# A hybrid decoder block on one core: weights ahead of x at the start, five low-part subtractions moved from GpSimd to VectorE, one weight split read from SBUF

## The chip, the cores and the metric

One core of a Trainium2 chip. The time is the device time of one execution in microseconds (us); less is better. Engines: PE (TensorE, matmuls; PEld are its weight loads), ACT (ScalarE), DVE (VectorE), POOL (GpSimd), SP (SyncE, which issues most transfers). SBUF is the on-chip memory, PSUM the matmuls' accumulators (8 banks).

## The reference, cut to what matters

```python
h = rms_norm(x, norm1_g)                 # x: 512 tokens x 2048
proj = h @ w_in                          # 2048 x 3840, split into head groups
out_a = dilated_mixture(aq, ak, av)      # A: 8 heads x 64
out_b = conformer_conv(bu, bg, ...)      # B: 512 channels
out_c = band_attention(cq, ck, cv, 127, sinks)  # C: 16 query heads, 2 kv heads
x = x + concat([out_a, out_b, out_c]) @ w_out   # 2048 x 2048
h2 = rms_norm(x, norm2_g)
x = x + (silu(h2 @ w_gate) * (h2 @ w_up)) @ w_down   # hidden width 5632
```

All in float32.

## The kernel before, in words

Everything is transposed: channels on the 128 partitions, 512 tokens in the free dimension. A float32 product is made of three matmuls in a reduced format (`mm3`): each operand is written as a rounded high part (a cast on ACT) and the low part that is left (a subtraction on DVE or POOL); high by high, and the two mixed products, are added up in PSUM.

The order of the work is the order in which the program is written; each engine takes its own instructions in that order. `Ticks` is a clock of the program's text: steps are put down for a later tick and written out between the matmuls.

Weights come in *units* of 128 x 1024 (the first two of 128 x 512). `pump` issues their transfers on SP's queue, `split_up_to(u)` writes the cast and the subtraction of all units up to u, and `next_unit` hands out the next one and splits two ahead (`SPLIT_AHEAD`). From the gate projection on the matrices are multiplied by a Strassen-like scheme of seven products, whose weight units are blocks and sums of blocks (`11`, `12`, `21`, `22`, `s`; the sums are made on POOL, L200). A unit there is cast twice on ACT: into PSUM (`wn`, L293), which the subtraction reads, and into SBUF (`wh`, L294), which PE reads. The first four units of that part are still split in the plain way (L289, L290), with one cast into SBUF.

The change touches four places:

- The start. `load_first(k)` loads 128 rows of x, `scaled` multiplies them by the norm's gain on ACT and makes the low part on DVE (L419, L420). The loop over `k` multiplies 16 such blocks into four PSUM banks `g4`, one for each 128 tokens, twelve matmuls a block; the square of x is summed on POOL.
- `split_mix`, which splits the attention's output rows (`mix_c0` and so on, 16 rows in the order of `ROWS`) into `mh_` and `ml_`. For the c rows the subtraction is on POOL (L865).
- `split_rows(k)`, which is called ahead of row k of the output projection and splits the rows k to k+2 that are there by then. `first_two` multiplies the first eight rows, all c rows, for two output tiles at once.
- The limit in `split_up_to` (L287) up to which units are split in the plain way: 93 units of the projections (`units`) and four more.

Around the second and third place ACT, DVE and POOL also do the attention of the A heads: exponentials (`e`), their sums on DVE (L775) and scaling on POOL (L779), transposes on PE (`a1t`), and the preparation of the last key and query tiles (`ak3`, `aq3`).

Of the kernel before, what the change touches and what calls it, by code (L numbers as in the profile page):

```python
# [9 lines left out]
F32 = mybir.dt.float32  # L10
F32R = mybir.dt.float32r
I32 = mybir.dt.int32
AF = mybir.ActivationFunctionType
ALU = mybir.AluOpType

P = 128
T = 512
NT = T // P
D = 2048
KT = D // P  # L20
# [28 lines left out]
ROWS = "c0 c1 c2 c4 c5 c3 c7 c6 a0 a1 b2 b1 b0 b3 a2 a3".split()  # L49
# [73 lines left out]
def kernel(ctx: ExitStack, tc: tile.TileContext, xT, wi, wo, wgu, wd, cst_in, outT):  # L123
    nc = tc.nc
# [20 lines left out]
    def slot(name, dt=F32, cols=T):  # L145
        return sp.tile([P, cols], dt, name=name, tag="s")

    def wide(i, name, dt=F32):
        return xp.tile([P, 2 * T], dt, name=name, tag=f"x{i}")
# [8 lines left out]
    units = [wi[0][:, :T], wi[0][:, T:]] + [wi[u] for u in range(1, 2 * N_IN)]  # L158
# [9 lines left out]
    def take(buf, key, n=1024):  # L168
        assert buf not in held
        held[buf] = key  # L170
        if buf[0] == "x":
            raws[key] = (wide(int(buf[1]), f"w{key}"), n)
        else:
            raws[key] = (wp.tile([P, 1024], F32, name=f"w{key}", tag=f"raw{buf}", bufs=1), n)
        return raws[key][0]

    def drop(key):
        for buf in [b for b, k in held.items() if k == key]:
            held.pop(buf)
        return raws.pop(key)  # L180
# [90 lines left out]
    def pump(limit):  # L271
        while at["entry"] < len(entries) and len(raws) < limit and entries[at["entry"]][0] not in held:
            buf, key, parts = entries[at["entry"]]
            (part,) = parts
            n = part.shape[-1] * (part.shape[1] if len(part.shape) == 3 else 1)
            t = take(buf, key, n)[:, :n]
            nc.sync.dma_start(t if len(part.shape) == 2 else t.rearrange("p (n c) -> p n c", n=part.shape[1]), part)
            at["entry"] += 1

    def split_up_to(i):  # L280
        while at["split"] <= min(i, len(works) - 1):
            key, last, eng = works[at["split"]]
            t, n = drop(key) if last else raws[key]
            u = at["split"]
            hi = wp.tile([P, 1024], F32R, name=f"wh{u}", tag="hi", bufs=SPLIT_BUFS)
            lo = wp.tile([P, 1024], F32R, name=f"wl{u}", tag="lo", bufs=SPLIT_BUFS)
            if eng or u < len(units) + 4:  # L287
                eng = eng or nc.vector
                nc.scalar.copy(hi[:, :n], t[:, :n])  # L289
                eng.tensor_sub(lo[:, :n], t[:, :n], hi[:, :n].bitcast(F32))  # L290
            else:
                near = psum["high"].tile([P, 1024], F32R, name=f"wn{u}", tag="h")
                nc.scalar.copy(near[:, :n], t[:, :n])  # L293
                nc.scalar.copy(hi[:, :n], t[:, :n])  # L294
                nc.vector.tensor_sub(lo[:, :n], t[:, :n], near[:, :n].bitcast(F32))  # L295
            splits[u] = (hi, lo)
            at["split"] += 1
# [5 lines left out]
    def next_unit(ahead=SPLIT_AHEAD):  # L303
        sums_now()
        u = at["use"]
        at["use"] += 1
        split_up_to(u + ahead)
        pump(RAW_EARLY if u < 20 else RAW_BUFS + N_WIDE)
        return splits.pop(u)

    def mm3(out, wh, wl, xh, xl, start, stop):
        nc.tensor.matmul(out, wh, xh, start=start, stop=False)  # L312
        nc.tensor.matmul(out, wh, xl, start=False, stop=False)  # L313
        nc.tensor.matmul(out, wl, xh, start=False, stop=stop)  # L314
# [6 lines left out]
    def load_first(k):  # L321
        x = slot(f"x{k}")
        nc.sync.dma_start(x, xT[k])
        xs.append(x)

    for k in range(X_AHEAD):
        load_first(k)
        u = k if k < 2 else k // 2 + 1
        if u < RAW_EARLY and (k < 2 or k % 2 == 0):
            pump(u + 1)  # L330
# [16 lines left out]
    def col(i):  # L347
        return cst[:, i:i + 1]
# [64 lines left out]
    def scaled(x, g, tag, k):  # L413
        if k < N_WIDE:
            both = wide(k, f"{tag}{k}", F32R)
            hi, lo = both[:, :T], both[:, T:]
        else:
            hi, lo = slot(f"{tag}h{k}", F32R), slot(f"{tag}l{k}", F32R)
        nc.scalar.activation(hi, x, AF.Copy, scale=g)  # L419
        nc.vector.scalar_tensor_tensor(lo, x, g, hi.bitcast(F32), op0=ALU.mult, op1=ALU.subtract)  # L420
        return hi, lo

    def add_square(acc, x, k, tag, eng=nc.gpsimd):
        if k == 0:
            nc.scalar.activation(acc, x, AF.Square)
        else:
            sq = slot(f"{tag}{k}")
            nc.scalar.activation(sq, x, AF.Square)  # L428
            eng.tensor_add(acc, acc, sq)  # L429
# [12 lines left out]
    g4 = [(column if j < COLUMN_BANKS - 1 else bank)(f"in{j}") for j in range(HEAD4)]  # L442
    h_hl = {}
    for k in range(2):
        h_hl[k] = scaled(xs[k], col(C_G1 + k), "h", k)
        split_up_to(k)
    pump(RAW_EARLY)
    add_square(ssum, xs[0], 0, "sq")
    for k in range(KT):
        if k + 2 < KT:  # L450
            h_hl[k + 2] = scaled(xs[k + 2], col(C_G1 + k + 2), "h", k + 2)
        if k < 2 or k % 2 == 0:
            wh, wl = next_unit()
            o = 0
        if k + X_AHEAD < KT:
            load_first(k + X_AHEAD)
        if k == 4:
            nc.sync.dma_start(cst[:, C_G2:], cst_in[:, C_G2:])
        if k + 1 < KT:
            add_square(ssum, xs[k + 1], k + 1, "sq")  # L460
        hi, lo = h_hl.pop(k)
        h_hi.append(hi)
        h_lo.append(lo)
        for i in range(NT):
            s = slice(i * P, (i + 1) * P)
            mm3(g4[i], hi[:, s], lo[:, s], wh[:, o:o + T], wl[:, o:o + T], k == 0, k == KT - 1)
        o += T
    xs = None
    c64 = cp.tile([P, NT], F32, name="c64")
# [79 lines left out]
    def ln_out(mix):  # L549
        b = spread(ln["r"], "lrs")  # L550
        for j in range(NB):
            nc.vector.tensor_mul(yconv[j], yconv[j], b)
        for j in range(NB):
            nc.scalar.activation(yconv[j], yconv[j], AF.Silu, bias=col(C_LB + j), scale=col(C_LG + j))
            mix[f"b{j}"] = yconv[j]
        for n, name in enumerate(r for r in ROWS if r[0] == "b"):
            ticks.after(1 + n, split_mix, name)
# [157 lines left out]
    def attention(kind, box, mix, mi, heads):  # L715
# [7 lines left out]
        def head(h):  # L723
# [107 lines left out]
            def out_rows(b):  # L831
                m = st["mix"]
                nc.vector.tensor_add(m[HALF[h]], m[HALF[h]], b[HALF[h]])
                if h == 1:
                    mix[mi] = m
                    if late:
                        ticks.after(1, split_mix, mi)
# [22 lines left out]
    def split_mix(name):  # L860
        if name not in m_hi:
            m = mix.pop(name)
            hi, lo = slot(f"mh_{name}", F32R), slot(f"ml_{name}", F32R)
            nc.scalar.copy(hi, m)
            (nc.gpsimd if name[0] == "c" else nc.vector).tensor_sub(lo, m, hi.bitcast(F32))  # L865
            m_hi[name], m_lo[name] = hi, lo

    vd = tc.dram_tile([NT, P, T], F32, name="vd")
# [9 lines left out]
    g4 = b = None  # L878
# [126 lines left out]
            operand(q, j, src)  # L1005

    def split_rows(k):
        for name in ROWS[k:k + 3]:
            if name in mix:
                split_mix(name)  # L1010

    def first_two(*ns):
        two = [((bank if i else column)(f"o0_{n}"), *next_unit(SPLIT_AHEAD - i)) for i, n in enumerate(ns)]
        for k in range(8):
            row = ROWS[k]
            while row not in m_hi and row not in mix:
                ticks.tick()
            split_rows(k)
            s = slice(k * P, (k + 1) * P)
            for b, wh, wl in two:  # L1020
                mm3(b, wh[:, s], wl[:, s], m_hi[row], m_lo[row], k == 0, k == 7)
            ticks.tick()
        for i, n in enumerate(ns):
            residual(n, two[i][0], 0)
            load_x(i + 2)
# [4 lines left out]
    for half in range(2):  # L1030
        for i, n in enumerate(OUT_ORDER[half]):
# [9 lines left out]
            wh, wl = next_unit()  # L1041
            if half == 1 and i == KT - 1:
                drop(first_sum[0][1])
            for kk in range(8):
                if half == 1 and i == KT - 2 and kk == 4:
                    first_sum[0][0]()
                k = 8 * half + kk
# [4 lines left out]
                s = slice(kk * P, (kk + 1) * P)  # L1052
# [345 lines left out]
    for g in range(2 * NP + N_DOWN):  # L1398
        t = g - 2 * NP
        turned = 0 <= t < N_TURNED  # L1400
        if t < 0:
            p, m = GU_ORDER[g // 2], g % 2
# [4 lines left out]
        for i, q in enumerate(ORDER):  # L1407
            sums_now()
            run(evacs)
            for sub in range(BY // 2 if turned else 1):  # L1410
                w = next_unit(SPLIT_AHEAD - (g == 0 and i == 2))
# [124 lines left out]
```

## Time and profile before

| | |
|---|---|
| three runs | 1879.63 us median, 1879.41 to 1881.6 |
| profiled execution | 1879.36 us, span 1877.5 us |
| PE busy | 1871.7 us, 9848 matmuls |
| DVE, ACT, POOL busy | 1454.1, 1343.7, 1217.0 us |
| chain that ended last | PE 96% of the span |
| granted TensorE clock | 1.0 |

A row of the timeline gives start and duration in us, the engine, the line of the kernel, the operation, what it writes and reads, and in brackets the idle time of the engine before it with what ended it. PE's records overlap by some tenths of a microsecond, since matmuls are pipelined.

### The profile page before, as it was taken

What the parts mean: (1) busy time and instruction counts of PE and PEld (TensorE: products, weight loads), DVE (VectorE), ACT (ScalarE), POOL (GpSimd) and SP (SyncE); (2) the same over time, 40 slices, a digit from 0 to 9 for tenths busy, and PEclk for the clock granted to TensorE, in tenths of its full rate; (3) what the DMA queues carried; (4) which work ended last, traced back from release to release, by engine and by line L of the source; (5) the groups of instructions that cost most, each with busy time, mean ns of one, the idle gap of its engine ahead of it and who ended that gap; (6) DMA issues with size and microseconds to landing.
All of it is one profiled execution on the core that took longest, in us unless ns stands there. A gap on an engine that the chain in (4) does not pass through costs nothing.

```text
span 1877.5 us, 28557 instructions
## 1 busy us (share of the span) xinstructions
PE 1871.7 (100%) x9848; PEld 1609.1 (86%) x9848; DVE 1454.1 (77%) x2376; ACT 1343.7 (72%) x1883; POOL 1217.0 (65%) x812
## 2 busy tenths in 40 slices
PE   9999999999999999999999999999999999999999
PEld 7888888888888888888888888888888888888888
DVE  7578999897679777777777777777777677778887
ACT  6246655553466887888878888888888887777675
POOL 5023444362155887778878877888787767766786
PEclk9999999999999999999999999999999999999999
DMA  7333233333342354443544445344455475578984
GB/s 271 122 109 102 81 105 102 121 107 138 113 146 89 114 178 142 163 163 132 184 134 164 162 137 181 132 166 160 145 175 196 151 237 185 196 253 283 311 241 124
DMA packets 157986, 301.09 MB, mean 160 GB/s; under 512 B 29968, under 2 KB 69008, under 8 KB 157840
## 3 DMA queue, kind: packets, MB, share of 16 engines
q1 hardware_dynamic: 157696, 299.25, 48.8%
q8 instruction: 78, 1.28, 0.3%
q14 instruction: 68, 0.56, 0.1%
q10 hardware_dynamic: 144, 0.01, 0.0%
HBM read 241.27 MB, written 50.33 MB: 155 GB/s over the span
## 4 chain that ended last, share of the span: by engine, by line
PE 96%; DVE 1%; issue 1%; ACT 1%; POOL 1%; DMA 0%; SPq 0%; DVEq 0%; POOLq 0%; ACTq 0%
PE out L1125 51%; PE out L1267 16%; PE o L313 3%; PE o L314 3%; PE o L312 3%; PE cq L312 1%; PE cq L313 1%; PE cq L314 1%; PE in L313 1%; PE ak L312 1%; PE bg L312 1%; PE ak L314 1%; PE ak L313 1%; PE bu L312 1%; PE bu L314 1%; PE bg L313 1%
## 5 line engine op out<-in xcount | busy, mean ns | idle before, releaser
L1125 PE MATMUL out<-h,wh 128*128 128x512 f32 x2464 | 588.4, 391 | 0.0
L1125 PEld LDWEIGHTS out<-h,wh 128*128 128x128 f32 x2464 | 452.7, 188 | 87.5
L1125 PEld LDWEIGHTS out<-h,wl 128*128 128x128 f32 x2464 | 316.2, 191 | 12.4 <-DVE wl L295 0.4
L1125 PE MATMUL out<-h,wl 128*128 128x256 f32 x2464 | 320.3, 283 | 0.2 <-DVE wl L295 0.2
L1267 PE MATMUL out<-wh,a 128*128 128x512 f32 x896 | 221.3, 389 | 0.0
L1267 PEld LDWEIGHTS out<-wh,a 128*128 128x128 f32 x896 | 168.2, 188 | 34.9
L289 ACT CAST wh<-w 128x1024 fp32r<-128x1024 f32 (+1 forms) x93 | 96.7, 1042 | 125.0 <-PE o L313 43.3
L290 DVE TENSOR_TENSOR wl<-w,wh 128x1024 fp32r<-128x1024 f32 (+1 forms) x93 | 117.2, 1262 | 46.7 <-ACT wh L289 45.7
L1267 PE MATMUL out<-wl,a 128*128 128x512 f32 x448 | 119.7, 389 | 0.0
L1267 PEld LDWEIGHTS out<-wl,a 128*128 128x128 f32 x448 | 84.1, 188 | 17.4
L513 DVE SCALAR_TENSOR_TENSOR y<-bu,cst,y 128x511 f32<-128x511 f32 (+14 forms) x120 | 90.3, 753 | 0.7
L1125 PE MATMUL out<-a,wh 128*128 128x512 f32 x330 | 80.1, 391 | 0.0
L1125 PEld LDWEIGHTS out<-a,wh 128*128 128x128 f32 x330 | 60.2, 188 | 11.4
L312 PE MATMUL o<-mh_c,wh 128*128 128x512 f32 x128 | 51.2, 400 | 0.0
L313 PE MATMUL o<-ml_c,wh 128*128 128x512 f32 x128 | 50.1, 392 | 0.4 <-POOL ml_c L865 0.3
L314 PE MATMUL o<-mh_c,wl 128*128 128x512 f32 x128 | 50.1, 391 | 0.0
L1312 DVE TENSOR_TENSOR Y<-Y,out 128x512 f32<-128x512 f32 x48 | 30.8, 683 | 19.0 <-PE out L1267 18.9
L1125 PEld LDWEIGHTS out<-a,wl 128*128 128x128 f32 x330 | 43.3, 191 | 2.2
L1125 PE MATMUL out<-a,wl 128*128 128x256 f32 x330 | 44.0, 283 | 0.0
L429 POOL TENSOR_TENSOR ssum<-ssum,sq 128x512 f32<-128x512 f32 x15 | 26.6, 1770 | 19.3 <-ACT sq L428 18.8
L312 PE MATMUL cq<-hh,wh 128*128 128x512 f32 x96 | 38.6, 402 | 0.0
L314 PE MATMUL cq<-hh,wl 128*128 128x512 f32 x96 | 37.5, 391 | 0.0
(3111 smaller groups left out, 5197.0 us busy)
## 6 DMA issues: line engine op xcount, KB each, us to landing
od<-a SPq DMA_DIRECT2D x140, 256.0 KB, 4.7
a<-od SPq DMA_DIRECT2D x140, 256.0 KB, 6.2
w<-in_wi SPq DMA_DIRECT2D x59, 512.0 KB, 3.6
w<-in_wo SPq DMA_DIRECT2D x32, 512.0 KB, 3.6
x<-in_xT SPq DMA_DIRECT2D x16, 256.0 KB, 6.7
xr<-in_xT SPq DMA_DIRECT2D x16, 256.0 KB, 3.8
x2d<-xr SPq DMA_DIRECT2D x16, 256.0 KB, 2.0
yd<-z SPq DMA_DIRECT2D x16, 256.0 KB, 5.5
```

The lines of the kernel that those rows point to most:

```text
L289: nc.scalar.copy(hi[:, :n], t[:, :n])
L290: eng.tensor_sub(lo[:, :n], t[:, :n], hi[:, :n].bitcast(F32))
L312: nc.tensor.matmul(out, wh, xh, start=start, stop=False)
L313: nc.tensor.matmul(out, wh, xl, start=False, stop=False)
L314: nc.tensor.matmul(out, wl, xh, start=False, stop=stop)
L429: eng.tensor_add(acc, acc, sq)
L513: nc.vector.scalar_tensor_tensor(yconv[j][:, i:], hconv[j][:, :T - i], c, yconv[j][:, i:], op0=ALU.mult, op1=ALU.add)
L1125: nc.tensor.matmul(out, lhs[:, s], rhs, start=begin, stop=last and low == flip[0] and x is xs[-1], skip_group_check=True)
L1267: nc.tensor.matmul(to[h], x[:, h * P:(h + 1) * P], v[:, j], start=sub == 0 and h not in started, stop=sub == 1 and n in (len(todo) - 1, le ...
L1312: nc.vector.tensor_add(t, t, b)
```

## The change

```diff
@@ split_up_to
-            if eng or u < len(units) + 4:
+            if eng or u < len(units) + 5:
@@ ahead of the loads of x
+    pump(1)
     for k in range(X_AHEAD):
         load_first(k)
@@ scaled
-        nc.scalar.activation(hi, x, AF.Copy, scale=g)
+        for s in (slice(0, P), slice(P, T)) if k == 0 else (slice(0, T),):
+            nc.scalar.activation(hi[:, s], x[:, s], AF.Copy, scale=g)
@@ the first two blocks
     for k in range(2):
+        split_up_to(k)
         h_hl[k] = scaled(xs[k], col(C_G1 + k), "h", k)
-        split_up_to(k)
@@ the loop over k
+        if k == 0:
+            for x, w in ((hi, wh), (hi, wl), (lo, wh)):
+                for i in range(NT):
+                    nc.tensor.matmul(g4[i], x[:, i * P:(i + 1) * P], w[:, :T], start=x is hi and w is wh, stop=False)
+            continue
         for i in range(NT):
             s = slice(i * P, (i + 1) * P)
-            mm3(g4[i], hi[:, s], lo[:, s], wh[:, o:o + T], wl[:, o:o + T], k == 0, k == KT - 1)
+            mm3(g4[i], hi[:, s], lo[:, s], wh[:, o:o + T], wl[:, o:o + T], False, k == KT - 1)
@@ split_mix
-            (nc.gpsimd if name[0] == "c" else nc.vector).tensor_sub(lo, m, hi.bitcast(F32))
+            (nc.gpsimd if name in ROWS[3:6] else nc.vector).tensor_sub(lo, m, hi.bitcast(F32))
@@ split_rows
-        for name in ROWS[k:k + 3]:
+        for name in ROWS[k:k + 4]:
```

`ROWS[3:6]` are c4, c5 and c3. The unit that the new limit takes in is block `12` of the first gate group (unit 97).

At the start the transfer of the first weights is issued ahead of x, and on ACT the casts of the first two units go ahead of the scaling of the first two blocks, the first of which is done in two pieces. ACT's instructions at the start of the program, before:

```order
L419 ACTIVATE h0_143<-x0_77,cst_75 128x512
L289 CAST wh0_146<-w0_79 128x512
L419 ACTIVATE h1_150<-x1_81,cst_75 128x512
L289 CAST wh1_153<-w1_83 128x512
L425 ACTIVATE ssum_138<-x0_77 128x512
L419 ACTIVATE h2_162<-x2_85,cst_75 128x512
L289 CAST wh2_165<-w2_87 128x1024
```

And of the change:

```order
L289 CAST wh0_143<-w0_77 128x512
L421 ACTIVATE h0_147<-x0_79,cst_75 128x128
L421 ACTIVATE h0_147<-x0_79,cst_75 128x384
L289 CAST wh1_151<-w1_83 128x512
L421 ACTIVATE h1_155<-x1_81,cst_75 128x512
L427 ACTIVATE ssum_138<-x0_79 128x512
L421 ACTIVATE h2_163<-x2_85,cst_75 128x512
L289 CAST wh2_166<-w2_87 128x1024
```

Each scaling of the first two blocks now stands behind a cast of weights. The matmuls of block 0 go through the four token groups once for each of the three products, and no longer through the three products for each group.

On DVE, ahead of the output projection, before (`wl63` is a weight unit's low part, `a1e` and `a2e` exponentials, `a2s` scores, `ak3` the last key tile):

```order
L290 TENSOR_TENSOR wl63_4120<-w63_3545,wh63_4119 128x1024
L750 ISA a2s01_4084,a2d0_3780<-a2s01_4084,bias_a_122 128x384
L750 ISA a2d0_3780 128x1
L753 SCALAR_TENSOR_TENSOR a2d0_3780<-a2d0_3780,aq2r_3921 128x1
L775 SCALAR_TENSOR_TENSOR a2e00_4159,a2d0_3780<-a2e00_4159,mult_a_121 128x128
```

And of the change:

```order
L290 TENSOR_TENSOR wl63_4121<-w63_3546,wh63_4120 128x1024
L872 TENSOR_TENSOR ml_c2_4128<-mix_c2_2447,mh_c2_4127 128x512
L757 ISA a2s01_4085,a2d0_3781<-a2s01_4085,bias_a_122 128x384
L757 ISA a2d0_3781 128x1
L760 SCALAR_TENSOR_TENSOR a2d0_3781<-a2d0_3781,aq2r_3922 128x1
L782 SCALAR_TENSOR_TENSOR a2e00_4164,a2d0_3781<-a2e00_4164,mult_a_121 128x128
```

The subtraction of c2 came in; those of c0 and c1 stand some twenty rows further up, those of c7 and c6 behind the two rows of `ak3` that follow (L635, now L642). POOL keeps c4, c5 and c3, which follow one another directly.

On DVE at the gate projection's first units, before (`out` are PSUM banks, `g1r` and `g1u` results of the first group):

```order
L1138 TENSOR_TENSOR g1r_6081<-g1r_6081,out0_5953 128x256
L1139 TENSOR_TENSOR g1r_6081<-g1r_6081,out0_5953 128x256
L295 TENSOR_TENSOR wl97_6086<-w('12', 'g1')_5686,wn97_6087 128x1024
L295 TENSOR_TENSOR wl98_6092<-w('22', 'g1')_5538,wn98_6093 128x1024
L1138 TENSOR_TENSOR g1u_6050<-g1u_6050,out3_5956 128x256
```

And of the change:

```order
L1145 TENSOR_TENSOR g1r_6082<-g1r_6082,out0_5954 128x256
L1146 TENSOR_TENSOR g1r_6082<-g1r_6082,out0_5954 128x256
L290 TENSOR_TENSOR wl97_6087<-w('12', 'g1')_5687,wh97_6086 128x1024
L295 TENSOR_TENSOR wl98_6091<-w('22', 'g1')_5539,wn98_6092 128x1024
L1145 TENSOR_TENSOR g1u_6051<-g1u_6051,out3_5957 128x256
```

Its place is the same; its second input is now `wh97` in SBUF, where it was `wn97` in PSUM, and ACT's cast of `wn97` is gone.

## The prediction

> **What bounds the kernel now.** I read the page first, then the timeline of the three places that the change touches: the first 13 us, the stretch from 390 to 414 us where the output projection begins, and the one from 577 to 609 us where the gate projection begins. Two lines of the page give the frame.
>
> ```profile
> span 1877.5 us, 28557 instructions
> PE 1871.7 (100%) x9848; PEld 1609.1 (86%) x9848; DVE 1454.1 (77%) x2376; ACT 1343.7 (72%) x1883; POOL 1217.0 (65%) x812
> ```
>
> TensorE (PE) is idle for 1877.5 - 1871.7 = 5.8 us of the whole span, and the change adds and removes no matmul. So nothing that it does elsewhere counts unless it moves a start on PE. An idle record is not the whole loss, though: matmul records overlap, so I read waits from start to start. Two matmuls with 512 columns that nobody holds up start 0.22 us apart (405.73 and 405.95 below).
>
> **Part 1, the first blocks of the input.** PE multiplies x in 16 blocks of 128 rows, twelve matmuls each; block k needs the cast weights `wh`, their low part `wl`, the scaled `h` and its low part. The rows are from the timeline: start, duration, engine, line, operation, and in brackets the idle time before with its releaser.
>
> ```profile
> 3.80 0.72 ACT L419 ACTIVATE h<-x,cst 128x512 fp32r<-128x512 f32 x1 [1.15 <-DMA cst<-in_cst]
> 4.56 0.75 DVE L420 SCALAR_TENSOR_TENSOR h<-x,cst,h 128x512 fp32r<-128x512 f32 x1 [2.90 <-ACT h L419]
> 4.59 0.62 ACT L289 CAST wh<-w 128x512 fp32r<-128x512 f32 x1
> 5.26 0.50 PE L312 MATMUL in<-wh,h 128*128 128x512 f32 x1
> 6.67 0.73 ACT L419 ACTIVATE h<-x,cst 128x512 fp32r<-128x512 f32 x1 [1.46 <-DMA x<-in_xT]
> 7.45 0.62 ACT L289 CAST wh<-w 128x512 fp32r<-128x512 f32 x1
> 8.11 0.69 DVE L290 TENSOR_TENSOR wl<-w,wh 128x512 fp32r<-128x512 f32 x1
> 8.66 0.39 PE L312 MATMUL in<-wh,h 128*128 128x512 f32 x1
> 9.40 1.05 ACT L289 CAST wh<-w 128x1024 fp32r<-128x1024 f32 x1 [0.18 <-DMA w<-in_wi]
> 10.48 1.22 DVE L290 TENSOR_TENSOR wl<-w,wh 128x1024 fp32r<-128x1024 f32 x1 [0.48 <-ACT wh L289]
> 11.49 0.39 PE L312 MATMUL in<-wh,h 128*128 128x512 f32 x1
> 11.76 0.50 PE L313 MATMUL in<-wl,h 128*128 128x512 f32 x1
> ```
>
> The last row is the last that is held up (it starts 0.06 after the row of 10.48, `wl` of the third unit, has ended at 11.70).
>
> Block 0 gains. The first weights now take the first place in the queue and x the second. The first place landed no later than 3.80, the second no later than 4.59. So the cast is over when x comes, and the scaling of 128 tokens and of the other 384 follows. For those widths I take the two forms of the exponentials on the same engine:
>
> ```profile
> L763 ACT ACTIVATE a2e<-a2s,a2d,aq2r 128x384 f32<-128x384 f32 x2 | 1.3, 670 | 0.0
> L763 ACT ACTIVATE a2e<-a2s,a2d,aq2r 128x128 f32<-128x128 f32 x2 | 0.9, 455 | 0.0
> ```
>
> The first piece is ready near 5.05, the rest near 5.6. PE starts one matmul at about 5.1 and goes on at 5.6; eleven more at 0.23 us end the block at about 8.2 instead of 8.66.
>
> Block 1 gives it back. Its cast is now ahead of its scaling on ACT, and the cast waits for a transfer that comes after x. From 6.67 (second x landed) to 9.40 (third weights landed) 1 MB came in three transfers, 256, 256 and 512 KB: 2.73 us, so 0.68 us for 256 KB, which puts the second weights at 7.35. Before, ACT used that time for the scaling and had both at 8.07. Now: cast 7.35 to 7.97, scaling to 8.7. On DVE `wl` ends at about 8.75, and the low part of h (0.75) at 9.5. The third matmul of the block needs it; ten more at 0.23 follow, so block 2 starts at about 11.85 instead of 11.49. Queued behind on ACT are the square of x (0.62), the next scaling (0.72) and the third cast (1.05), each starting about 0.1 before its forerunner's end: cast done at 10.75, `wl` at about 12.0 instead of 11.70. So PE's last held-up matmul moves from 11.76 to about 12.05. **Term: +0.3 us.** If the second weights land at once after x, at 6.67, the third cast still waits for its data at 9.40, and the term is -0.1; if all of ACT's shift (7.45 + 0.62 + 0.73 = 8.80) reaches PE it is +0.6.
>
> **Part 2, the low parts of the c rows.** Eight subtractions on GpSimd (POOL) become three there and five on DVE. Rows of the three engines, in order of time:
>
> ```profile
> 392.91 1.29 POOL L865 TENSOR_TENSOR ml_c<-mix_c,mh_c 128x512 fp32r<-128x512 f32 x1
> 392.93 1.68 DVE L775 SCALAR_TENSOR_TENSOR a1e<-a1e,mult_a 128x384 f32<-128x384 f32 x1
> 399.04 2.62 POOL L779 TENSOR_SCALAR a1e<-a1e,a1d 128x512 f32<-128x512 f32 x1
> 400.98 0.29 DVE L775 SCALAR_TENSOR_TENSOR a2e<-a2e,mult_a 128x128 f32<-128x128 f32 x1
> 401.63 4.43 POOL L865 TENSOR_TENSOR ml_c<-mix_c,mh_c 128x512 fp32r<-128x512 f32 x3
> 402.46 0.47 PE L312 MATMUL o<-mh_c,wh 128*128 128x512 f32 x1
> 403.07 0.50 PE L313 MATMUL o<-ml_c,wh 128*128 128x512 f32 x1
> 403.10 1.19 DVE L753 SCALAR_TENSOR_TENSOR a2d<-a2d,aq2r 128x1 f32<-128x1 f32 x1
> 404.81 1.52 DVE L635 SCALAR_TENSOR_TENSOR ak<-ak3raw,gqk,ak3t 64x512 f32<-64x512 f32 x2
> 405.73 0.39 PE L313 MATMUL o<-ml_c,wh 128*128 128x512 f32 x1
> 405.95 0.39 PE L314 MATMUL o<-mh_c,wl 128*128 128x512 f32 x1
> 406.48 0.63 PE L795 MATMUL a1t<-ident,a1e 128*128 128x128 f32 x4
> 411.91 1.29 POOL L865 TENSOR_TENSOR ml_c<-mix_c,mh_c 128x512 fp32r<-128x512 f32 x1
> 412.11 1.10 DVE L580 TENSOR_TENSOR aq3v<-aq3v,c 128x8 f32<-128x8 f32 x1
> 412.56 0.40 PE L312 MATMUL o<-mh_c,wh 128*128 128x512 f32 x1
> 413.14 0.68 DVE L865 TENSOR_TENSOR ml_a<-mix_a,mh_a 128x512 fp32r<-128x512 f32 x1
> 413.25 0.50 PE L313 MATMUL o<-ml_c,wh 128*128 128x512 f32 x1 [0.28 <-POOL ml_c L865]
> ```
>
> PE loses time at three starts: 403.07 (0.61 after 402.46, so 0.38 beyond 0.23) and 413.25 (0.69, so 0.46), both for a subtraction on POOL (of c2 and of c6), and 406.48 (0.53, so 0.30), where transposes start just after DVE's L635 ended at 406.33. They overwrite a PSUM bank, and I take L635, which reads `ak3t` out of PSUM, to be what frees it. Together that is 1.14 us, all that this edit can win.
>
> On DVE a subtraction costs 0.68 (413.14). It also takes collisions away. A DVE operation of one column took 1.19 us while POOL subtracted, and one of eight columns 1.10. The overlaps are 1.27 us (392.93 to 394.20) and 1.09 (412.11 to 413.20); both go, since c0 and c6 leave POOL. The one at 403.10 stays: POOL still does c4, c5 and c3 in a row from about 401.6.
>
> Up to L635 DVE gets three more (c0, c1, c2): 3 x 0.68 - 1.27 = +0.77. About half of it vanishes in the wait at 403.10, which ends with POOL's row and not with DVE's. So L635 ends 0.3 us later, near 406.65, and the transposes start at 406.8. The stall at 403.07 goes (c2 is ready on DVE by about 401), but the bank takes it back and 0.3 more. The stall at 413.25 goes, since c7 and c6 follow L635 on DVE by 410. **Term: +0.3 - 0.46 = -0.15 us.** Behind the five subtractions are queued the exponentials' sums and the weight splits on DVE; the latter have the collisions taken away (1.09) against c7 and c6 (1.36). The fourth row, split with the first three, costs ACT nothing in sum. Bounds: -1.1 if all three stalls go; above, see the second rival.
>
> [...] POOL's L779 ran from 399.04 to 401.66, and DVE's L775, with two inputs in SBUF, ran through in 0.29 us meanwhile: no blocking by that kind of POOL operation. [...]
>
> **Part 3, block 12 without its PSUM copy.** ACT casts once instead of twice, about 1 us that nobody waits for there. The low part on DVE then reads both inputs from SBUF.
>
> ```profile
> 577.98 2.41 POOL L200 TENSOR_TENSOR w('21', 'g1')_5483<-w('21', 'g1')_5483,w('11', 'g1')_5585 128x1024 f32<-128x1024 f32 x1
> 578.07 3.39 DVE L290 TENSOR_TENSOR wl<-w,wh 128x1024 fp32r<-128x1024 f32 x1
> 605.00 2.40 POOL L200 TENSOR_TENSOR w('s', 'g1')_5737<-w('s', 'g1')_5737,w('12', 'g1')_5686 128x1024 f32<-128x1024 f32 x1
> 605.35 1.21 DVE L295 TENSOR_TENSOR wl<-w('12', 'g1')_5686,wn 128x1024 fp32r<-128x1024 f32 x1
> 607.65 1.11 PE L1125 MATMUL out<-h,wl 128*128 128x256 f32 x8
> 608.92 0.62 PE L1125 MATMUL out<-h,wl 128*128 128x256 f32 x3 [0.16 <-DVE wl L295]
> ```
>
> With `wn` in PSUM the split ran in 1.21 us under POOL's addition of 605.00. At 578.07 the same operation from SBUF, started 0.09 after such an addition, took 3.39 us and ended 1.07 after it. The new split starts at the same place, 0.35 after the addition. So it ends at 607.40 + 1.07 = 608.47 instead of 606.56, and PE's eight matmuls of 607.65 start at about 608.5. The next split follows with 1.21 us, to 609.7, and PE's matmuls of 608.92 start then. **Term: +0.75 us**, between -0.2 (no collision, and the wait of 0.16 goes too) and +1.1. [...]
>
> **Sum.** +0.3 - 0.15 + 0.75 = +0.9 us. The profiled execution took 1879.36 us, of which 1877.5 is the span; the median of the three runs is 1879.63 (1879.41 to 1881.6). From the median: 1880.5 us. A difference of 0.2%, 3.8 us, is about what a measurement of this kernel can tell from no change.
>
> **Rivals.**
>
> The edits pay and nothing takes their place: the split of block 12 gets in ahead of POOL's addition or passes it, and the bank at 406.48 comes free earlier as c0 leaves POOL. Then -0.1 - 1.1 - 0.2 = -1.4 us, 1878.2. For it: POOL's three subtractions at 401.63 start no later. Against: the addition of 605.00 starts 0.35 us ahead of the split, and 578.07 shows what happens then. 25%.
>
> VectorE becomes the bound before L635 (the slower side). If POOL, relieved of c0 and c1, is ahead of DVE at the next scaling and then at c4 and c5, DVE's operations with two SBUF inputs wait for it one after the other: 3 x 0.68 = 2.04, no collision saved, and one more of 1.29 (a POOL row) added, less 0.4 of slack: +2.9 at L635, and PE's transposes start 2.9 later. With +0.3 and +0.75 that is +3.95, 1883.6. It decides over 0.2% once L635 is 2.7 us later than before. For it: DVE has hardly any idle time there, as the rows show its operations back to back with collisions. Against: L775 at 400.98. [...] 18%, half of it beyond 0.2%.
>
> The head start does not come at all, since PE's first matmul still waits for x: then the start is 0 to +0.6, which is inside the forecast.
>
> **How the numbers follow.** Forecast 57%: 1880.5. The range goes down to 1878.0, the first rival less 0.2 for the runs' scatter, and up to 1883.0, which leaves out the upper half of the second rival. Faster by over 0.2% would need more than all the stalls that the change touches (0.1 + 1.1 + 0.2): 3% for something not seen. Slower by over 0.2%: half of the second rival, and 3% for the scatter: 12%. Within: 85%.
>
> **What would show it.** Right: PE's matmul of block 2 on `wl` at about 12.05; the start on c2's low part not held up, that on c6 neither; transposes a1t at 406.5 to 407.1, counted with the shift of the start; DVE's split of block 12 lasting over 2.5 us and PE held up at the eight matmuls by about 0.9. Wrong: a cast of the second weights before 7.0; a split of 1.2 us at block 12; a stall of over 1 us on c2, or on the transposes that wait for L635.

## The result, and the profile after

The changed kernel takes 1882.78 us (median of 20 runs, 1881.32 to 1883.26), the kernel before 1879.26 (20 runs beside them, 1878.9 to 1881.6). The ratio is 1.0016, with a 95% interval of 1.0010 to 1.0022: slower, and by 3.5 us between the medians, which is within the 0.2% that the prediction called no change. The forecast was 1880.5, the range went up to 1883.0.

The profiled execution took 1882.03 us. Its page begins:

```profile
span 1880.2 us, 28559 instructions
PE 1871.5 (100%) x9848; PEld 1609.0 (86%) x9848; DVE 1458.3 (78%) x2381; ACT 1342.7 (71%) x1883; POOL 1211.3 (64%) x807
```

The span grew by 2.7 us, and PE was busy for 0.2 us less. So all of it is waiting. The table of waits of PE names the places (engine, line, what was waited for, us in total, times, longest):

```profile
PE a1t L802 <- DVE ak L642: 2.5, 1, 2.5
PE out L1132 <- DVE wl L290: 0.7, 1, 0.7
PE in L312 <- ACT h L421: 0.6, 1, 0.6
```

They are the change's three places. In the timeline (start, duration, engine, line, operation, idle time before), first the start:

```profile
5.03 1.47 PE L469 MATMUL in<-wh,h 128*128 128x512 f32 x4
7.60 0.62 ACT L289 CAST wh<-w 128x512 fp32r<-128x512 f32 x1 [2.12 <-DMA w<-in_wi]
8.13 0.72 ACT L421 ACTIVATE h<-x,cst 128x512 fp32r<-128x512 f32 x1
8.90 0.50 PE L312 MATMUL in<-wh,h 128*128 128x512 f32 x1 [0.55 <-ACT h L421]
12.31 0.41 PE L313 MATMUL in<-wl,h 128*128 128x512 f32 x1
```

The first product started 0.23 us earlier, at 5.03. The second weights landed no later than 7.60, and block 1's scaling, now behind their cast, was ready at 8.85; PE waited for it. The row of 12.31, the first matmul of block 2 on its `wl`, stood at 11.76 before: 0.55 late.

The second place, in order of time:

```profile
396.89 1.67 POOL L592 TENSOR_TENSOR ak3r<-ak3v,nhalf 128x8 f32<-128x8 f32 x1 [0.43 <-DVE ak3v L587]
399.37 1.58 POOL L786 TENSOR_SCALAR a1e<-a1e,a1d 128x512 f32<-128x512 f32 x1 [0.82 <-DVE a1d L784]
399.54 1.60 DVE L290 TENSOR_TENSOR wl<-w,wh 128x1024 fp32r<-128x1024 f32 x1
400.91 4.44 POOL L872 TENSOR_TENSOR ml_c<-mix_c,mh_c 128x512 fp32r<-128x512 f32 x3
401.06 1.78 DVE L872 TENSOR_TENSOR ml_c<-mix_c,mh_c 128x512 fp32r<-128x512 f32 x1
403.40 0.60 DVE L760 SCALAR_TENSOR_TENSOR a2d<-a2d,aq2r 128x1 f32<-128x1 f32 x1
404.14 1.50 DVE L782 SCALAR_TENSOR_TENSOR a2e<-a2e,mult_a 128x256 f32<-128x256 f32 x1
405.99 0.40 PE L314 MATMUL o<-mh_c,wl 128*128 128x512 f32 x1
407.24 1.52 DVE L642 SCALAR_TENSOR_TENSOR ak<-ak3raw,gqk,ak3t 64x512 f32<-64x512 f32 x2
408.90 0.63 PE L802 MATMUL a1t<-ident,a1e 128*128 128x128 f32 x4 [2.52 <-DVE ak L642]
```

The stalls of 403.07 and 413.25 are gone, 0.38 + 0.46 us. In their place the transposes of `a1t` start 2.91 us after the matmul ahead of them; before it was 0.53. Sum: 2.38 - 0.84 = +1.54 us. DVE's own rows say why. Three operations stand under POOL's three subtractions, which lasted from 400.91 to 405.35: c2's took 1.78 us where the same operation took 0.68 at 413.14 before, L760 0.60, L782 1.50. Before, the rows of these last two lines took 0.16 and 0.43; the power on POOL (`ak3r`, a norm to the power -0.5, which comes ahead of its scaling and subtractions) and the last weight split on DVE stood thus:

```profile
397.38 1.67 POOL L585 TENSOR_TENSOR ak3r<-ak3v,nhalf 128x8 f32<-128x8 f32 x1
399.08 1.22 DVE L290 TENSOR_TENSOR wl<-w,wh 128x1024 fp32r<-128x1024 f32 x1
400.87 0.16 DVE L753 SCALAR_TENSOR_TENSOR a2d<-a2d,aq2r 128x1 f32<-128x1 f32 x1
401.44 0.43 DVE L775 SCALAR_TENSOR_TENSOR a2e<-a2e,mult_a 128x256 f32<-128x256 f32 x1 [0.16 <-ACT a2e L763]
```

And the third place:

```profile
606.86 2.39 POOL L200 TENSOR_TENSOR w('s', 'g1')_5738<-w('s', 'g1')_5738,w('12', 'g1')_5687 128x1024 f32<-128x1024 f32 x1
607.22 3.12 DVE L290 TENSOR_TENSOR wl<-w('12', 'g1')_5687,wh 128x1024 fp32r<-128x1024 f32 x1
607.59 2.09 PE L1132 MATMUL out<-h,wh 128*128 128x512 f32 x8
610.39 1.87 PE L1132 MATMUL out<-h,wl 128*128 128x256 f32 x12 [0.71 <-DVE wl L290]
```

The split started 0.36 us after POOL's addition, took 3.12 us instead of 1.21. Eight matmuls at 0.24 us from 607.59 would have let the next start at 609.51; it started at 610.39, 0.87 us late, and before, counted in the same way, 0.21 (608.92): +0.66. Counted so, the three places sum to 0.55 + 1.54 + 0.66 = 2.75 us, the whole of the longer span.

These are readings at the waits. A matmul that had to wait is followed by the next one some 0.1 us late as well (from 413.25 to 413.58 before), so what lasts is seen by comparing one matmul in both kernels a little behind each place. PE is 0.47 us late behind the start (12.56 against 12.09), 1.86 behind the c rows (415.44 against 413.58) and 2.59 behind block 12 (612.57 against 609.98). So the start lasts with 0.47, the c rows with 1.39 and block 12 with 0.73.

The median rose by 0.8 us more than the span of this one execution. Of the 20 runs, 12 have a mean granted clock of 0.999 (1882.55 to 1883.26 us) and 8 one of 1.0 (1881.32 to 1882.85); the profiled one is of the second group. The kernel before had 1.0 in each of the 101 runs that stood beside the experiments. One run of the start with block 1 in its old order (see below) took 2046.99 us at a clock of 0.851 and is left out of that kernel's ratio.

### The profile page after: what moved, and what is told of

The parts are those of the page before. It is cut to its first block, busy times and chain, and to the rows that moved or that the text cites. A ratio compares the mean times of both kernels' runs of the same rounds, so it can differ in the third digit from the quotient of the medians.

```text
span 1880.2 us, 28559 instructions
## 1 busy us (share of the span) xinstructions
PE 1871.5 (100%) x9848; PEld 1609.0 (86%) x9848; DVE 1458.3 (78%) x2381; ACT 1342.7 (71%) x1883; POOL 1211.3 (64%) x807
## 4 chain that ended last, share of the span: by engine, by line
PE 96%; DVE 3%; issue 0%; ACT 0%; DMA 0%; SPq 0%; POOL 0%; DVEq 0%; ACTq 0%; POOLq 0%
PE out L1132 51%; PE out L1274 16%; PE o L312 3%; PE o L313 3%; PE o L314 3%; PE cq L312 1%; PE cq L313 1%; PE cq L314 1%; PE ak L312 1%; PE ak L314 1%; PE bg L312 1%; PE ak L313 1%; PE bu L312 1%; PE bg L314 1%; PE bu L314 1%; PE bg L313 1%
```

## The experiments

Each was timed beside the kernel before, in three series whose medians for it were 1879.4, 1879.3 and 1879.3 us. Line numbers are those of each kernel: L635 and L642 are the same line. Only for the c rows alone and for the filled wait does the interval of the ratio leave out 1; what is said of the others rests on the rows of their profiles, and their medians are given with it.

**The start alone.**

```diff
+    pump(1)
     for k in range(X_AHEAD):
...
     for k in range(2):
+        split_up_to(k)
         h_hl[k] = scaled(xs[k], col(C_G1 + k), "h", k)
-        split_up_to(k)
```

with block 0 in two pieces and its matmuls by product, as in the change.

> Only the start of the change (first weights ahead of x, block 0 in two pieces and in three passes, both casts ahead of both scalings); the rest as before. Theory A, the cast of the second weights holds up ACT and with it block 1: PE's first matmul of block 1 waits about 0.6 us, block 2's matmul on the low part of the weights is at about 12.3 us (11.76 before), the span is 0.5 to 0.6 us longer. Rival: block 0's gain survives, 0.0 to 0.4 us shorter. On the granted clock: if it is the start that made it 0.999 in most runs of the change, it does so here (median then about 2 us above before); if it is the wait of 2.5 us in the output projection, the clock is 1.0 here in nearly all runs.

Measured: 1879.57 us, ratio 1.0001 (0.9992 to 1.0009), span 1877.9, every run at a clock of 1.0. Block 2's matmul on `wl` started at 12.02 in this profile, 0.26 later than before. That is neither theory's figure: PE's first matmul of block 1 did not wait (8.97), since the second weights landed at 7.29 here, not at 7.60, and block 0's first four matmuls took 2.15 us where they took 1.47 in the change. The start costs some tenths of a microsecond at most, and not the clock.

**The c rows alone.**

```diff
-            (nc.gpsimd if name[0] == "c" else nc.vector).tensor_sub(lo, m, hi.bitcast(F32))
+            (nc.gpsimd if name in ROWS[3:6] else nc.vector).tensor_sub(lo, m, hi.bitcast(F32))
...
-        for name in ROWS[k:k + 3]:
+        for name in ROWS[k:k + 4]:
```

> Only the c rows (five subtractions on VectorE, three on GpSimd, split four rows ahead). Theory A, GpSimd's three subtractions in a row and VectorE's operations with two SBUF inputs shut each other out, and the key tile's scaling comes 2.4 us late: the transposes of a1t start 2.0 to 2.4 us later than before, the span is 1.3 to 1.7 us longer. Rival, only VectorE's added work counts (3 x 0.68 = 2.0 less the collision that goes, 1.2): 0.3 us later, span 0.1 to 0.3 us shorter. On the granted clock: if this wait of PE lets the clock go down, most runs show 0.999 and the median is 2.5 to 3 us above before; if not, it is 1.0 and the median moves with the span.

Measured: 1882.09 us, ratio 1.0014 (1.0005 to 1.0022), span 1880.1. Most of the loss, 2.7 of 3.5 us by the medians, is in this part, and that is what was expected if the wait brings the clock down. Nine of the 11 runs have a clock of 0.999 (1881.59 us and up), the two others 1.0 and the two lowest times (1880.54, 1880.78). The profiled one is of the nine. Its timeline shows the same wait, and what follows it:

```profile
405.15 0.40 PE L314 MATMUL o<-mh_c,wl 128*128 128x512 f32 x1
408.08 1.04 PE L795 MATMUL a1t<-ident,a1e 128*128 128x128 f32 x4 [2.54 <-DVE ak L635]
410.63 0.63 PE L314 MATMUL o<-mh_c,wl 128*128 128x512 f32 x1
411.05 0.63 PE L312 MATMUL o<-mh_c,wh 128*128 128x512 f32 x1
411.76 0.39 PE L314 MATMUL o<-mh_c,wl 128*128 128x512 f32 x1
```

Four transposes take 1.04 us here and 0.63 in the changed kernel's own profile; matmuls start 0.42 us apart, until near 411.5. The windows of this run (stretch, its length, busy times, then the granted clock in the column PEclk) show that the clock was down:

```profile
404.00:407.00 3.00, 1.54 (x8) 0.93 (x6) 2.93 (x8) 1.97 (x4) 2.33 (x3) 1.00 0.00 1
407.00:410.00 3.00, 1.92 (x9) 1.95 (x10) 2.92 (x7) 0.59 (x1) 0.20 (x1) 0.69 0.76 163
410.00:413.00 3.00, 3.00 (x14) 2.43 (x14) 2.68 (x8) 2.99 (x6) 1.25 (x1) 0.74 0.83 230
413.00:416.00 3.00, 3.00 (x15) 2.50 (x14) 2.86 (x11) 0.10 (x1) 0.00 (x0) 1.00 0.00 0
```

So after this wait of 2.5 us PE ran at half speed for 3.4 us (408.08 to about 411.5). Half of 3.4 us in 1880 is 0.0009, just the 0.999 of the run's mean. The other runs with 0.999 were not profiled; that they had the same stretch is inferred from this figure.

**Block 12 alone.**

```diff
-            if eng or u < len(units) + 4:
+            if eng or u < len(units) + 5:
```

> Only block 12 without its PSUM copy. Theory A, the split waits for GpSimd's addition: it takes about 3.1 us, PE's matmuls on it are held up about 0.9 us, the span is 0.6 to 0.7 us longer. Rival, the collision is a matter of the shift of 2 us that the other edits made: 1.2 us, and the span 0.1 to 0.2 us shorter.

Measured: 1880.13 us, ratio 1.0003 (0.9995 to 1.0012), span 1878.6, clock 1.0 in all runs. The split took 3.12 us under POOL's addition again:

```profile
605.61 3.12 DVE L290 TENSOR_TENSOR wl<-w('12', 'g1')_5686,wh 128x1024 fp32r<-128x1024 f32 x1
608.78 2.36 PE L1125 MATMUL out<-h,wl 128*128 128x256 f32 x16 [0.72 <-DVE wl L290]
```

The collision doesn't depend on what the two other parts shift. By their medians the three parts alone give +0.2, +2.7 and +0.7 us, together 3.6; the change gave 3.5.

**The start with block 1 in its old order.** Only the first cast goes ahead of its scaling:

```diff
     for k in range(2):
-        split_up_to(k)
+        split_up_to(0)
         h_hl[k] = scaled(xs[k], col(C_G1 + k), "h", k)
+        split_up_to(k)
```

> The start of the change, but in block 1 the scaling stands ahead of the cast again, as before; block 0 as in the change. Theory A (the order on ACT in block 1 is what costs): block 1 starts at about 8.3 us without a wait of its first matmul, the low part of the third weights, which wait for their transfer, ends at about 11.7 as before, and the span is within 0.2 us of before. Rival (x comes one place later in the queue, or the passes of block 0 cost): the span is 0.4 to 0.6 us longer, as with both casts ahead.

Measured: 1879.24 us, ratio 0.9999 (0.9990 to 1.0007), span 1877.0. In its profile block 1 started at 8.24 without a wait, as expected, and the matmul that the kernel before has at 12.09 stood at 11.44, earlier than expected: the second weights landed at 6.50. The time is 0.3 below the start alone, the direction expected, but neither can be told from the kernel before.

**All c rows on VectorE.**

```diff
-            (nc.gpsimd if name[0] == "c" else nc.vector).tensor_sub(lo, m, hi.bitcast(F32))
+            nc.vector.tensor_sub(lo, m, hi.bitcast(F32))
...
-        for name in ROWS[k:k + 3]:
+        for name in ROWS[k:k + 4]:
```

> All eight rows' low parts are subtracted on VectorE, split four rows ahead as in the change; nothing of the start or of block 12 is changed. Theory A (in the change VectorE's L290, L865, L760 and L782 were late because GpSimd's subtractions of 1.4 to 1.7 us, which with this edit began ahead of them, held them up): without any such subtraction each low part takes VectorE about 0.7 us alone, L760 0.29 and L782 about 0.8 instead of 0.61 and 1.50, L635 and L642 are at most 0.9 us late, the first a1t transpose waits under 1.0 us instead of 2.5, the granted clock stays at 1.0 there, and the span is 1877.0 to 1878.3 (before: 1877.5). Theory B (VectorE simply has more to do in these 13 us, whoever else works): three more subtractions of 0.68 us stand ahead of L642, the first a1t transpose waits 3.5 us or more, the clock falls behind it, and the span is 1880.5 or more.

Measured: 1879.96 us, ratio 1.0004 (0.9995 to 1.0012), span 1878.2, clock 1.0 in all 11 runs. The rows that had been held up ran quiet, as theory A had it; the transposes still waited 1.68 us, more than A allowed and far less than B:

```profile
399.13 1.61 DVE L290 TENSOR_TENSOR wl<-w,wh 128x1024 fp32r<-128x1024 f32 x1
400.67 1.28 DVE L865 TENSOR_TENSOR ml_c<-mix_c,mh_c 128x512 fp32r<-128x512 f32 x2
402.51 0.16 DVE L753 SCALAR_TENSOR_TENSOR a2d<-a2d,aq2r 128x1 f32<-128x1 f32 x1
402.59 1.29 DVE L865 TENSOR_TENSOR ml_c<-mix_c,mh_c 128x512 fp32r<-128x512 f32 x2
404.01 0.42 DVE L775 SCALAR_TENSOR_TENSOR a2e<-a2e,mult_a 128x256 f32<-128x256 f32 x1
406.00 1.52 DVE L635 SCALAR_TENSOR_TENSOR ak<-ak3raw,gqk,ak3t 64x512 f32<-64x512 f32 x2
407.66 0.63 PE L795 MATMUL a1t<-ident,a1e 128*128 128x128 f32 x4 [1.68 <-DVE ak L635]
```

Both theories had a part. VectorE's way from the start of the last weight split (399.13 here, 399.54 in the changed kernel) to that of L635 was 5.73 us long before, 7.70 in the change, and is 6.87 here, with four subtractions more at 0.6 us each from start to start. So three subtractions on GpSimd cost VectorE 0.83 us more than having them itself. In the change only c2's 0.60 us is new work on this way. Taken from start to start, its rows give +2.98 of new hold-ups (the split 0.38, c2 1.10, L760 0.42, L782 1.08) and +0.60 for c2, against -1.03 for the hold-up of 403.10, which is gone, and -0.58 at two short waits that VectorE had before: +1.97.

**The engine choice without the fourth row.** The first hunk of the c rows alone; split three rows ahead as before.

> Of the rows' edit only the choice of the engine: three c rows' low parts on GpSimd, the other two on VectorE, but split three rows ahead as in the kernel before instead of four. Theory A (what makes L642 late is that GpSimd, freed of two early rows, begins its three subtractions before VectorE is through with its own): GpSimd's three still stand beside VectorE's L760 and L782, and the first a1t transpose waits 1.5 to 3 us, span 1879 to 1880.5. Rival (splitting one row farther ahead puts one more subtraction of VectorE's ahead of L642, and that is what makes it late): without it the wait is under 1 us and the span 1877.0 to 1878.2.

Measured: 1879.95 us, ratio 1.0004 (0.9995 to 1.0013), span 1877.8, clock 1.0 in all runs. The wait is 1.67 us, as theory A had it, and the rival is out; the span was lower than A's, since the stalls of c2 and c6 are gone (0.84 us) and this profile's start was 0.4 us early (see the last section). So the engine choice makes L635 late by itself: VectorE's way is 6.86 us long, though c2's subtraction, which began 0.08 us ahead of POOL's, ran quiet in 0.68. The fourth row turns 1.67 us of waiting into 2.54, with which the lower clock comes.

**Block 12 one unit earlier.**

```diff
-            if eng or u < len(units) + 4:
+            if eng or u < len(units) + 5:
...
-                w = next_unit(SPLIT_AHEAD - (g == 0 and i == 2))
+                w = next_unit(SPLIT_AHEAD)
```

and the raw block is kept until POOL's addition has read it.

> Block 12 is summed without its PSUM copy as in the change, but the weights' low part wl97 is subtracted at the place in the order that the other units have, one unit earlier, ahead of the opening unit's addition on GpSimd instead of beside it; nothing of the start or of the rows is changed. Theory A (the 3.12 us of that subtraction are GpSimd's addition L200 beside it): it takes 1.1 to 1.7 us, PE does not wait for it at L1132, and the span is 1877.1 to 1877.6, the 0.2 us of PE's loss at block 12 in the kernel before being gone. Theory B (the operands' place or the order around block 12 makes it long by itself): it takes about 3 us again, PE waits 0.5 us or more somewhere in the third product's first blocks, and the span is 1878.2 or more.

Measured: 1880.26 us, ratio 1.0005 (0.9996 to 1.0014), span 1879.1. The split is quiet, as theory A said, but the span is not lower:

```profile
604.39 1.21 DVE L290 TENSOR_TENSOR wl<-w('12', 'g1')_5686,wh 128x1024 fp32r<-128x1024 f32 x1
605.52 0.15 DVE L438 TENSOR_SCALAR n2v<-n2s 128x4 f32<-128x4 f32 x1
605.75 1.02 POOL L439 TENSOR_TENSOR n2r<-n2v,nhalf 128x4 f32<-128x4 f32 x1 [16.92 <-DVE n2v L438]
606.83 0.65 PE L369 MATMUL n2s<-ident,n2r 128*128 128x128 f32 x4 [0.68 <-POOL n2r L439]
```

It stood ahead of the norm's row L438 on VectorE, which POOL's power and then PE's transposes wait for. I had overlooked that: a new wait of 0.68 us took the old one's place, and it is not all (see the next run).

**Block 12 behind L438.**

```diff
                 (norm2a, norm2b)[i - 2]()
+                if i == 2:
+                    split_up_to(at["use"] - 1 + SPLIT_AHEAD)
```

with the limit of `+ 5` and the raw block kept as in the run before.

> Block 12 without its PSUM copy, and its weights' low part subtracted right behind the norm's L438 on VectorE: later than in the run with the split one unit earlier, where it held up L438, and ahead of GpSimd's addition L200, unlike the change. Theory (the two costs seen so far, 0.9 us beside L200 and 0.8 us ahead of L438, are all there is): the subtraction takes 1.2 to 1.3 us beside GpSimd's 1.0 us power, no wait of TensorE at L369 or L1125 over 0.1 us, the 0.2 us of loss in the kernel before gone, span 1877.2 to 1877.5. Rival (the subtraction is held up by GpSimd's power as well, or ends under L200): it takes 2 us or more, and the span is 1878.0 or more.

Measured: 1880.18 us, ratio 1.0006 (0.9997 to 1.0015), span 1878.2. The split is quiet again, and PE waits again, 0.46 us:

```profile
603.82 0.15 DVE L438 TENSOR_SCALAR n2v<-n2s 128x4 f32<-128x4 f32 x1
603.88 1.21 DVE L290 TENSOR_TENSOR wl<-w('12', 'g1')_5686,wh 128x1024 fp32r<-128x1024 f32 x1
604.04 1.93 POOL L439 TENSOR_TENSOR n2r<-n2v,nhalf 128x4 f32<-128x4 f32 x1 [15.79 <-DVE n2v L438]
606.03 0.65 PE L369 MATMUL n2s<-ident,n2r 128*128 128x128 f32 x4 [0.46 <-POOL n2r L439]
```

Now POOL is the one held up: its power took 1.93 us instead of 1.02, under a split that had started 0.16 earlier. The rival had the hold-up but on the other side; it goes both ways. The wait of PE is not the whole loss at either place. Compared matmul by matmul with the kernel before, PE falls back 0.49 us by 610 us in the run one unit earlier and 0.25 here, and between 617 and 625 us another 0.46 and 0.43, which the table of waits doesn't name. There it meets weights whose cast on ACT has only just ended (618.66 and 617.82); that cast stood behind an operation that had waited for POOL, whose addition L200 began 1.1 and 0.9 us later than PE's own delay would put it. At each of the three places tried, the split from SBUF cost 0.7 to 0.9 us by the median, and the kernel before, with the second cast into PSUM, has none of it.

**The wait filled.** The changed kernel with nine more matmuls ahead of the transposes that wait (they add one product of row c4 nine times more, so the output is no longer the reference's):

```diff
                 mm3(b, wh[:, s], wl[:, s], m_hi[row], m_lo[row], k == 0, k == 7)
+            if k == 3:
+                for _ in range(9):
+                    nc.tensor.matmul(two[0][0], two[0][1][:, s], m_hi[row], start=False, stop=False)
```

> The changed kernel, with nine more 128x512 matmuls on TensorE right ahead of the a1t transposes that wait 2.5 us for L642 (row c4's first product is added nine times more, which spoils that output block and moves nothing else). They take about 9 x 0.23 = 2.1 us and fit into the wait. Theory A (an idle time of 2.5 us lets the granted clock halve for some us in most runs, beside the wait itself): TensorE is idle for 0.4 us only, the span is that of the change within 0.2 us (1880.2), every run has a clock of 1.0, and the median comes down by about 1 us to 1881.2 to 1881.8. Rival (the clock of 0.999 and the upper group of times have another cause, such as the chip or where the work stands in time): most runs are at 0.999 again and the median is 1882.5 or more.

Measured: 1881.71 us (1880.87 to 1882.15), ratio 1.0011 (1.0002 to 1.0020), span 1879.7, clock 1.0 in all 11 runs.

```profile
405.52 0.40 PE L314 MATMUL o<-mh_c,wl 128*128 128x512 f32 x1
405.76 2.21 PE L1031 MATMUL o<-mh_c,wh 128*128 128x512 f32 x9
408.44 0.63 PE L802 MATMUL a1t<-ident,a1e 128*128 128x128 f32 x4 [0.48 <-DVE ak L642]
```

More work on PE, and 1.07 us less time; the median is about that of the change's own eight runs with a clock of 1.0 (1881.58). The span is 0.5 us below that of the change's profile because the start was that much earlier (405.52 against 405.99). The transposes still start 2.92 us after the last matmul of the rows (2.91 in the change); what is gone is the half clock behind them. So it is PE's idle time that brought the clock down here (0.999 in 12 of 20 runs with the wait, in none of 11 with it filled), not the place in the program. The chip alone isn't it either: on the chip of the c rows alone, the start alone and block 12 alone had 1.0 in every run. That the chip has a part is not excluded, since the series ran on three chips and the unfilled change was not timed on this one.

**Only the two late rows on VectorE.**

```diff
-            (nc.gpsimd if name[0] == "c" else nc.vector).tensor_sub(lo, m, hi.bitcast(F32))
+            (nc.gpsimd if name[0] == "c" and name not in ROWS[6:8] else nc.vector).tensor_sub(lo, m, hi.bitcast(F32))
```

> Of the rows' edit only what moves c7 and c6 from GpSimd to VectorE, with the split three rows ahead and GpSimd's first subtractions as in the kernel before; nothing else. Theory (only what is put ahead of L642 on VectorE or beside it on GpSimd costs; c7 and c6 come behind it): the a1t transposes lose 0.3 us as before, the wait of 0.45 us at 413.25 in the kernel before is gone, span 1876.9 to 1877.2, time 0.3 to 0.6 below the kernel before. Rival (the subtractions on VectorE delay what stands behind them, the a2e scaling and a1pl, as much as they save): span 1877.4 or more and no difference in time.

Measured: 1879.09 us, ratio 1.0 (0.9991 to 1.0008), span 1876.8. The stall at c6 is gone and the transposes lose 0.32 us as before, so the edit does what the theory says; the start of this profile was 0.35 us early, which leaves 0.35 of the 0.7 us to it. Its runs lie in two groups, seven at 1878.42 to 1879.11 and four at 1880.47 to 1880.88; why is open, and the kernel before has such runs too (three of the 33 beside it, at 1881.29 to 1881.49). The difference can't be told from nothing.

**Two combinations.** The start in its mended form and the two late rows, with block 12 one unit earlier in the first and behind L438 in the second:

> Three edits together: the start of the change with block 1's scaling left ahead of its cast, on the rows only c7 and c6 subtracted on VectorE with the split three rows ahead as in the kernel before, and block 12 with its weights' low part one unit earlier. By the theory that the collisions cost the change its time: 0.5 us less at the start (measured alone), 0.3 to 0.8 less at the rows, since the two late subtractions no longer stand beside L782, and 0.2 less at block 12, a span of 1876.0 to 1876.6 and a time of 1878.0 to 1878.5, 0.9 to 1.4 below the kernel before. By the rival that any subtraction moved to VectorE makes L642 late: the a1t transposes wait 1.5 us or more and the time is 1879.5 or more.

Measured: 1879.63 us, ratio 1.0002 (0.9993 to 1.0011), span 1878.2. The rows paid, and block 12 took it back by what its own run showed.

> The start of the change with block 1's scaling left ahead of its cast, c7 and c6 alone on VectorE, and block 12 with its subtraction right behind L438. By the theory the parts add up: 0.1 to 0.5 less at the start, 0.3 to 0.6 less at the rows, 0.0 to 0.2 less at block 12, so a time 0.5 to 1.2 below the kernel before. By the rivals of the two runs beside it, or if the start's gain was an accident of when the data landed, the time is that of the kernel before within 0.3.

Measured: 1879.32 us, ratio 0.9999 (0.9990 to 1.0008), span 1877.8. The same, with the smaller wait. No version beats the kernel before by what the runs can tell. The start and the late rows without block 12 were not run together.

## Why the prediction was right or wrong

The time lies in the range and within the 0.2%, and the forecast was 2.3 us too low. That it lies inside, 0.2 us under the upper end, is partly luck: the range reached that far only for the lower half of the second rival, whose mechanism was the one at work, and the clock's 1.1 us stood in no term. The prediction's own sign of being wrong, a stall of over 1 us on the transposes that wait for L635, did come.

*The start, forecast +0.3.* Right in mechanism in the change's profile: block 0 gained (5.03), block 1 gave it back behind its cast. That profile has +0.55 (0.47 of it lasts), the run of this part alone 0.26 at the same matmul, there without the wait; both are inside the bounds of -0.1 to +0.6. The landing of the second weights, put at 7.35, came at 7.60 in the change and at 7.29 and 6.50 in the two runs of the start. Two profiles don't settle such a size, see the last section.

*The c rows, forecast -0.15.* This is the step that failed. The two stalls went, as forecast. What was wrong is "about half of it vanishes in the wait at 403.10", with POOL doing c4, c5 and c3 "from about 401.6": counted from the weight split ahead of it, L642 was 2.0 us later, not 0.3 (399.54 to 407.24 against 399.08 to 404.81). I had counted the collisions that go when c0 and c6 leave POOL, and held POOL's other work where it was. It moved. Without c0 and c1 its power began 2.65 us ahead of that weight split instead of 1.70; the scaling behind it, 0.17 us ahead of the split instead of 0.04, was through in 1.58 us instead of 2.62; and the three subtractions began 1.37 us behind the split instead of 2.55, ahead of c2's, L760 and L782. The second rival had just that mechanism (POOL "ahead of DVE at the next scaling and then at c4 and c5"), with +2.9 for L635, a total of 1883.6, and 18%. Against it I had put one row, L775 at 400.98, which ran through beside POOL's scaling. That row is about a TENSOR_SCALAR; it says nothing of POOL's subtractions, and my own row of 403.10 did.

Where both operations had two inputs in SBUF, the one that began first held the other up in these rows: c2's subtraction took 1.78 us when it began 0.15 us behind a POOL subtraction (401.06 behind 400.91, in the change) and 0.68 when it began 0.08 ahead of one (the engine choice without the fourth row), and POOL's power took 1.93 us instead of 1.02 when it began 0.16 behind a VectorE split. With POOL's scaling, which has one, it was not so: the weight split that began 0.17 us behind it took 1.60 us, where waiting for its end at 400.95 would have made it some 2.6 (an estimate: 1.41 of waiting and the 1.22 of the row before), and L775 ran through in 0.29.

*The clock.* No step of the prediction had it. Twelve of the 20 runs have a mean clock of 0.999, the figure of the one such profile (the c rows alone), which shows 3.4 us at half clock right behind the 2.5 us wait, and filling the wait gave back 1.07 us. Of the 2.6 us that the forecast lacks (+3.5 against +0.9), about 1.5 are the c rows (+1.39 against -0.15) and 1.1 the clock; the start (0.2 by the median of its own runs) takes 0.1 off, and block 12 came as forecast.

*Block 12, forecast +0.75.* Right: 0.73 in the change, +0.7 alone by the medians, a split of 3.12 us as forecast from the row of 578.07 (3.39). The first rival, that the split passes the addition, is out.

*Beyond 0.2%.* "Once L635 is 2.7 us later" left out the clock: with it, 2.0 us brought the medians 0.19% apart.

## What to carry to other kernels

Taking work off an engine moves all that is queued behind it earlier: write down what it will then stand beside, before counting what the edit saves. VectorE operations with two inputs in SBUF and GpSimd's two-input operations held each other up here, whichever came first, by about what the other had left to run (the split by 1.9 us of the addition's 2.0, the power by 0.9 us of the split's 1.05). So such an operation cost most of its neighbour's length here (1.9 of 2.39 us, 0.9 of 1.21), and the PSUM copy that looked superfluous was what avoided it (1.21 us beside the same addition). A wait of 2.5 us on TensorE was worse than its length here (filled, it gave back 1.07 us), waits of 1.7 us were not (clock 1.0 in all 22 runs): keep it short, or fill it.

## What the runs showed of the hardware that I had not expected

The granted clock fell to half after 2.5 us without matmuls, for about 3.4 us in the one profile that shows it (the c rows alone: 0.69 in the mean from 407 to 410 us, 0.74 from 410 to 413, matmuls 0.42 us apart and then 0.23 again), and the mean clock was 0.999 in 12 of 20 runs of the change and 9 of 11 of the c rows alone; after waits of 1.67 and 1.68 us, on another chip than the latter, in none of 22 (all at 1.0). Why only some of the runs have it, no run shows.

The start varies by itself. In eight profiles with the start unchanged, PE's row of `c0o` that waits 0.2 to 0.3 us for `c0pl` came at 157.65 to 158.49 us, with the same program up to there. In the kernel before, the input's matmuls were 0.23 us apart from 6.33 on; in the run with block 12 one unit earlier, whose start is the same, they were still 0.43 apart at 6.94:

```profile
6.51 0.63 PE L314 MATMUL in<-wh,h 128*128 128x512 f32 x1
6.94 0.63 PE L312 MATMUL in<-wh,h 128*128 128x512 f32 x1
7.36 0.53 PE L313 MATMUL in<-wl,h 128*128 128x512 f32 x1
```

So 0.8 us between two spans can be the start alone, and a term of 0.3 us there is read from the medians or not at all.
